# A two-block sequence mixer on one core: the weight loads issued by ScalarE instead of SyncE

## The chip, the core and the metric

The kernel runs on one core of a Trainium2 chip. A core has TensorE (PE in the profile; its weight loads are PEld), VectorE (DVE), ScalarE (ACT), GpSimd (POOL) and SyncE (SP), which run their own instruction streams in order and wait for each other through semaphores. The metric is the device time of one execution in microseconds, from the kernel's launch to its end; the comparison uses the median of several executions.

## What the reference computes

The input x has 2048 positions of 1024 channels in float32. The first block normalizes it, projects it, runs a diagonal state-space scan on 512 channels and a short gated convolution on the other 512, projects back and adds. The second block is a bidirectional chunked state-space mixer with a Fourier branch, and then a gated feed-forward network of width 2816. Cut to its frame:

```python
def reference(x, ...):
    xn = rmsnorm(x, norm_gain)
    proj = xn @ w_in                                    # 1024 -> 3072
    y = concat([s5_mixer(u, ...) * silu(z), short_conv_mixer(h, b, c, conv_w) * silu(z2)])
    x = rmsnorm(x + y @ w_out, final_norm_gain)         # end of the first block
    hc = modulate(rms_norm(ctx, g), shift, scale)       # 256 positions of context
    _, hf, hb = ssd_bidir(conv7(hc @ w_in2), ...)       # its two final states
    hx = modulate(rms_norm(x, g), shift, scale)
    y = ssd_bidir(conv7(hx @ w_in2), ..., hf, hb)       # states and outputs, chunks of 128
    x = x + gm * rms_norm(concat([fourier_mix(uf), rms_norm(y * silu(z))]) @ w_out2)
    hx2 = modulate(rms_norm(x, g), shift, scale)
    return x + gf * rms_norm((silu(hx2 @ w_gate) * (hx2 @ w_up)) @ w_down)
```

## The kernel before

Activations lie with channels on the 128 partitions, in four blocks of 512 positions. Nearly all of the multiplying is done in tiles of 128 output channels by 512 positions. `mtile` makes such a tile: `weights` fetches a strip of the weight matrix (128 x 1024 float32, 512 KB; strips of `w_down` are narrower), and `gemm` multiplies it with eight strips of the activations. To keep float32 accuracy each operand is split into a high and a low part of TensorE's fp32r type: `whi` is ScalarE's rounding of the raw strip `wraw` (L112), `wlo` the remainder, computed by VectorE or, in some stages, by GpSimd (L115, chosen by `pool_lo`). A full tile is 24 matmuls in this order: sixteen that use `whi` (L126 with the high part of the activations, L127 with the low part), then eight that use `wlo` (L130). There are 634 strips in one execution.

The buffers around a strip set its pace. `wraw` has three buffers, `whi` and `wlo` two each. So the load of strip j can start once `wlo` of strip j-3 has been computed; the rounding of strip j once the L127 matmuls of strip j-2 are done; and `wlo` of strip j once its L130 matmuls are done. PSUM holds three buffers for these tiles (`mm`), two for small results (`nb`) and three for the state and scan products (`ss`).

The order of the work is not written out by hand. The Python code lists units of work (`a1_units`, `s5_units`, `b_units` and so on), `weave` and `merge` interleave them, and a scheduler then orders the instructions on each engine; `high_priority(offset=self.ahead)` lets it bring the three steps of `weights` forward by some 40 to 75 places. The stages that matter here, in the profiled execution:

- 0 to about 1090 us: the first block. Beside the weight tiles run the state-space parameters (many small DVE operations, tables `T` on POOL, stores of `Cd`, `Gd`, `Td`, `Md`) and the scan (`s5_units`), which loads those tables again.
- about 1090 to 1640 us: `b_units`, the projection of the second block, the seven-tap convolution and the chunk states. A chunk's states are four products on PE (L1125), each into an `ss` buffer; VectorE adds the first half into `hF` (L1299) and ScalarE copies the second half into `stB` (L1301). The fourth product needs the buffer of the first one again. Here `wlo` is computed by POOL for the first three of the four blocks.
- about 1640 us to the end: the attention-like part of the chunks, the output projection, and the feed-forward network, one block of positions woven into the next.

All 2037 transfers are issued by SyncE, in one line. Every transfer signals one of eight semaphores, which are taken in turn (`DMAHW0` to `DMAHW7` in the listings below), and a transfer waits for the one that used its semaphore before, unless that is known to have ended.

Of the kernel before, what the change touches and what calls it, by code (L numbers as in the profile page):

```python
# [61 lines left out]
class Kernel:  # L62
# [41 lines left out]
    def weights(self, src, pool=None, bufs=2):  # L104

        nc = self.nc
        n = src.shape[1]
        with self.tc.high_priority(offset=self.ahead):
            raw = self.t(self.wp, (P, n), "wraw", bufs=3)
            nc.sync.dma_start(out=raw, in_=src)  # L110
            hi = self.t(pool or self.wp, (P, n), "whi", F32R, bufs=bufs)
            nc.scalar.copy(hi, raw)  # L112
            lo = self.t(pool or self.wp, (P, n), "wlo", F32R, bufs=bufs)
            eng = nc.gpsimd if self.pool_lo else nc.vector
            eng.tensor_tensor(lo, raw, hi.bitcast(F32), ALU.subtract)  # L115
        return hi, lo
# [1841 lines left out]
```

## Time and profile before

| What | Value |
|---|---|
| time of three executions | 3629.4, 3638.18 and 3636.63 us, median 3636.63 us |
| profiled execution | 3634.7 us, of which its span from first to last instruction is 3632.8 us |
| mean granted clock of TensorE | 0.98 |
| busy share of the span | PE 95%, PEld 78%, DVE 59%, ACT 40%, POOL 27% |
| memory | 472.63 MB read, 112.36 MB written, 161 GB/s over the span |

The profiled execution lies 1.9 us below the median. A share of busy time is an average over stages with different limits, and issuing a transfer is not counted as busy.

### The profile page before, as it was taken

To read this page: it belongs to the slowest core of one execution; us is meant where nothing else is said; L and a number is where in the kernel's file an instruction comes from. 1 tells how busy PE (TensorE), PEld (TensorE's weight loads), DVE (VectorE), ACT (ScalarE), POOL (GpSimd) and SP (SyncE) were. 2 spreads that over 40 slices of the span, in tenths; PEclk is the share of its full clock that TensorE was granted. 3 is DMA by queue.
4 is the path that set the end of the run, shared out by engine and by line. 5 is a ranking of instruction groups with operands and counts; after the bars stand their busy time and mean duration, and the time that the engine had idled before them with its cause. 6 is when DMAs were issued, how large, how long until landed. Compare 5 with 4: busy or idle time off the path is not lost.

```text
span 3632.8 us, 46986 instructions
## 1 busy us (share of the span) xinstructions
PE 3462.0 (95%) x16602; PEld 2831.0 (78%) x16602; DVE 2147.9 (59%) x3991; ACT 1461.9 (40%) x2350; POOL 965.3 (27%) x931
## 2 busy tenths in 40 slices
PE   8899999988989999999999999999999999999998
PEld 6677888776778888876777788877888778887887
DVE  8765534446687577777756544566445664454334
ACT  3233232234444344335535533355333553343222
POOL 1764233232353453343213101131011220110001
PEclk9999999999989999999999999999999999999999
DMA  6467565677654565466554334443345443444232
GB/s 199 156 190 223 191 210 175 203 230 241 211 191 153 178 204 172 163 205 203 164 186 137 118 111 155 155 149 120 111 135 171 140 130 111 127 153 130 83 113 76
DMA packets 322508, 588.14 MB, mean 162 GB/s; under 512 B 73952, under 2 KB 150624, under 8 KB 321376
## 3 DMA queue, kind: packets, MB, share of 16 engines
q1 hardware_dynamic: 322272, 585.13, 51.1%
q8 instruction: 132, 2.16, 0.2%
q14 instruction: 104, 0.85, 0.1%
HBM read 472.63 MB, written 112.36 MB: 161 GB/s over the span
## 4 chain that ended last, share of the span: by engine, by line
PE 60%; DVE 6%; DMA 4%; ACT 2%; issue 1%; POOL 1%; SPq 0%; POOLq 0%; DVEq 0%; ACTq 0%
PE mm L130 17%; PE mm L126 17%; PE mm L127 17%; PE ss L1125 1%; PE nb L940 1%; PE ss L1473 1%; PE ss L1523 1%; DVE cy L1038 1%; DMA outT<-n_t 1%; PE nb L1501 1%; PE ss L1138 1%; PE mm L1149 1%; PE mm L1150 0%; PE mm L1151 0%; PE nb L192 0%
## 5 line engine op out<-in xcount | busy, mean ns | idle before, releaser
L112 ACT CAST whi<-wraw 128x1024 fp32r<-128x1024 f32 (+3 forms) x634 | 568.9, 898 | 1044.3 <-PE mm L127 758.0
L115 DVE TENSOR_TENSOR wlo<-wraw,whi 128x1024 fp32r<-128x1024 f32 (+3 forms) x516 | 538.2, 1044 | 698.2 <-PE mm L130 487.3
L126 PE MATMUL mm<-xh,whi 128*128 128x512 f32 (+1 forms) x2000 | 801.2, 403 | 49.4 <-ACT whi L112 30.1
L127 PE MATMUL mm<-xl,whi 128*128 128x512 f32 (+1 forms) x2000 | 787.8, 396 | 5.8 <-DVE xl L142 3.6
L152 POOL TENSOR_TENSOR n_acc<-n_acc,n_sq 128x512 f32<-128x512 f32 (+1 forms) x175 | 229.5, 1315 | 1365.5 <-ACT n_sq L151 1337.9
L126 PE MATMUL mm<-dxh,whi 128*128 128x512 f32 x1408 | 549.9, 391 | 1.7 <-ACT dxh L997 1.7
L127 PE MATMUL mm<-dxl,whi 128*128 128x512 f32 x1408 | 548.6, 390 | 1.6 <-DVE dxl L998 1.5
L130 PE MATMUL mm<-xh,wlo 128*128 128x512 f32 (+1 forms) x2000 | 500.2, 392 | 9.9 <-DVE wlo L115 9.6
L126 PEld LDWEIGHTS mm<-xh,whi 128*128 128x128 f32 x2000 | 385.7, 193 | 138.7 <-ACT whi L112 40.9
L127 PEld LDWEIGHTS mm<-xl,whi 128*128 128x128 f32 x2000 | 385.7, 193 | 86.1 <-DVE xl L142 6.6
L130 PEld LDWEIGHTS mm<-xh,wlo 128*128 128x128 f32 x2000 | 375.7, 191 | 89.9 <-DVE wlo L115 12.9
L115 POOL TENSOR_TENSOR wlo<-wraw,whi 128x1024 fp32r<-128x1024 f32 (+1 forms) x118 | 284.1, 2410 | 549.0 <-ACT whi L112 268.0
L130 PE MATMUL mm<-dxh,wlo 128*128 128x512 f32 x1408 | 349.7, 389 | 0.0
L126 PEld LDWEIGHTS mm<-dxh,whi 128*128 128x128 f32 x1408 | 264.1, 188 | 57.7 <-ACT dxh L997 3.0
L127 PEld LDWEIGHTS mm<-dxl,whi 128*128 128x128 f32 x1408 | 264.3, 188 | 57.2 <-DVE dxl L998 2.8
L130 PEld LDWEIGHTS mm<-dxh,wlo 128*128 128x128 f32 x1408 | 263.6, 188 | 54.3
L126 PE MATMUL mm<-hh,whi 128*128 128x512 f32 (+1 forms) x744 | 285.5, 390 | 5.0 <-ACT hh L141 4.7
L1038 DVE SCALAR_TENSOR_TENSOR cy<-mm,vecs,cy 128x504 f32<-128x504 f32 (+5 forms) x396 | 266.9, 690 | 27.6 <-ACT cy L1032 24.4
L127 PE MATMUL mm<-hl,whi 128*128 128x512 f32 (+1 forms) x744 | 280.5, 382 | 2.0 <-DVE hl L142 2.0
L130 PE MATMUL mm<-hh,wlo 128*128 128x512 f32 (+1 forms) x744 | 199.3, 383 | 0.0
L126 PEld LDWEIGHTS mm<-hh,whi 128*128 128x128 f32 x744 | 139.7, 189 | 36.7 <-ACT hh L141 9.4
L127 PEld LDWEIGHTS mm<-hl,whi 128*128 128x128 f32 x744 | 140.5, 189 | 30.4 <-DVE hl L142 5.2
(473 smaller groups left out, 4510.7 us busy)
## 6 DMA issues: line engine op xcount, KB each, us to landing
wraw<-w_in SPq DMA_DIRECT2D x186, 512.0 KB, 4.5
wraw<-w_gate SPq DMA_DIRECT2D x88, 512.0 KB, 3.7
wraw<-w_up SPq DMA_DIRECT2D x88, 512.0 KB, 3.6
wraw<-w_out SPq DMA_DIRECT2D x64, 512.0 KB, 3.9
mraw<-w_ada SPq DMA_DIRECT2D x96, 256.0 KB, 3.7
n_x<-xT SPq DMA_DIRECT2D x85, 256.0 KB, 4.7
n_x<-X1d SPq DMA_DIRECT2D x80, 256.0 KB, 4.0
n_x<-X2d SPq DMA_DIRECT2D x72, 256.0 KB, 4.0
```

The lines of the kernel that those rows point to most:

```text
L112: nc.scalar.copy(hi, raw)
L115: eng.tensor_tensor(lo, raw, hi.bitcast(F32), ALU.subtract)
L126: nc.tensor.matmul(ps, lhsT=hi[:, s], rhs=xh, start=k == ks[0], stop=False)
L127: nc.tensor.matmul(ps, lhsT=hi[:, s], rhs=xl, start=False, stop=False)
L130: nc.tensor.matmul(ps, lhsT=lo[:, s], rhs=rhs(k)[0], start=False, stop=k == ks[-1])
L152: nc.gpsimd.tensor_tensor(acc, acc, sq, ALU.add)
L940: nc.tensor.matmul(ps, lhsT=raws[k // 4][:, k % 4 * P:(k % 4 + 1) * P], rhs=sc[:, k, 0:n], start=k == 0, stop=k == KD - 1)
L1038: nc.vector.scalar_tensor_tensor(yr[:, :, lo:hi], pr[:, :, lo + d:hi + d], w(k), yr[:, :, lo:hi], ALU.mult, ALU.add)
L1125: nc.tensor.matmul(ps, lhsT=B_tm[:, c, g], rhs=xw[:, g].rearrange("p d r e -> p (d r e)"), start=True, stop=True)
L1138: nc.tensor.transpose(ps[:, c], src[:, c * P:(c + 1) * P], self.ident)
L1149: nc.tensor.matmul(ps, lhsT=ah, rhs=wh[:, s], start=(k == 0), stop=False)
L1473: nc.tensor.matmul(ps, lhsT=CT[:, g, c * P:(c + 1) * P], rhs=hFB[:, g].rearrange("p d e -> p (d e)"), start=True, stop=True)
```

## The change

One word of `weights`: the transfer of the raw strip is put into ScalarE's instruction stream instead of SyncE's. Nothing else in the source differs, and no buffer is added.

```diff
@@ -107,7 +107,7 @@
         n = src.shape[1]
         with self.tc.high_priority(offset=self.ahead):
             raw = self.t(self.wp, (P, n), "wraw", bufs=3)
-            nc.sync.dma_start(out=raw, in_=src)
+            nc.scalar.dma_start(out=raw, in_=src)
             hi = self.t(pool or self.wp, (P, n), "whi", F32R, bufs=bufs)
             nc.scalar.copy(hi, raw)
             lo = self.t(pool or self.wp, (P, n), "wlo", F32R, bufs=bufs)
```

The 634 strip loads leave SyncE's stream (2033 transfers in its listing before, 1401 now, four of them pieces of `w_uf` that use the same raw buffers) and enter ScalarE's. Since the scheduler decides again, the other engines' orders move too, most of all in the first fifth of the program. Three places, as the built programs list them; a row is line, operation, output<-inputs with buffer numbers, and size, and in brackets the semaphores that it waits for (named by the engine that signals them).

The first is the start of ScalarE's stream, as one piece of the difference. `n_x` and `n_t` are strips of x, `xh` their high parts, `sc` a small vector.

```order
-L329 ACT_TABLE_LOAD
-L329 ACTIVATE sc_6_104<-vecs_1_75 128x16
+L110 DMA wraw_47_220<-w_in 128x1024
+L110 DMA wraw_66_291<-w_in 128x1024
+L762 ACT_TABLE_LOAD
+L762 ACTIVATE xh_18_127<-n_x_22_131,vecs_1_75 128x512
 L112 CAST whi_48_222<-wraw_47_220 128x1024
-L762 ACTIVATE xh_18_127<-n_x_22_131,vecs_1_75 128x512
```

The function table that stood ahead of everything is replaced by another one, which stands with the first `xh`; the table and the vector `sc` that stood first now come six `xh` later. With its waits the new table load reads:

```order
L762 ACT_TABLE_LOAD [waits DMAHW2_49]
L762 ACTIVATE xh_18_127<-n_x_22_131,vecs_1_75 128x512 [waits DMAHW1_49]
L112 CAST whi_48_222<-wraw_47_220 128x1024 [waits DMAHW0_49]
```

So it stands behind a wait for a load from SyncE, where the old one waited for nothing.

The second place is in the first block, where the output projection begins. SyncE's stream before, with the load of strip 1242 between a store of the previous tile's sum (`X2d<-us`, which waits for DVE) and others:

```order
L698 DMA s5C_1217_6372<-Cd_98 128x1024 [waits DMAHW7_49,PE_49]
L700 DMA s5M_1218_6374<-Md_99 128x512
L199 DMA n_x_1220_6406<-xT 128x512 [waits DMAHW2_49,DMAHW1_49,DVE_49]
L902 DMA X2d_87<-us_1215_6366 128x512 [waits DVE_49]
L110 DMA wraw_1242_6513<-w_out 128x1024 [waits DMAHW3_49,Pool_49]
```

And ScalarE's stream of the change around the same load:

```order
L884 ACTIVATE hs_1188_6239<-mm_1187_6226,hb_glu_5_102 128x512 [waits Activation_49]
L110 DMA wraw_1228_6447<-w_out 128x1024 [waits DMAHW4_49,Pool_49]
L110 DMA wraw_1242_6513<-w_out 128x1024 [waits DMAHW6_49,Pool_49]
L141 CAST xh_1131_5998<-zs_1189_6241 128x512 [waits DVE_49]
L112 CAST whi_1222_6410<-wraw_1221_6408 128x1024 [waits DMAHW5_49,PE_49]
```

The load no longer stands behind that store and those loads; it stands ahead of the rounding of an earlier strip, and waits for POOL (the `wlo` that frees its buffer) and for a semaphore.

The third place is a chunk's states, on ScalarE. Before:

```order
L112 CAST whi_2094_10568<-wraw_2093_10566 128x1024 [waits DMAHW5_49,PE_49,Pool_49]
L1032 ACTIVATE cy_2064_10427<-mm_2063_10402,vecs_1_75 128x512 [waits PE_49]
L1301 COPY stB_2069_10447<-ss_2070_10448 128x192 [waits DMAHW5_49,DVE_49,Activation_49]
L1301 COPY stB_2069_10447<-ss_2071_10452 128x192 [waits DVE_49]
L1301 COPY stB_2069_10447<-ss_2072_10456 128x192 [waits DVE_49]
```

Of the change:

```order
L112 CAST whi_2094_10568<-wraw_2093_10566 128x1024 [waits DMAHW5_49,PE_49]
L1032 ACTIVATE cy_2064_10427<-mm_2063_10402,vecs_1_75 128x512 [waits PE_49]
L110 DMA wraw_2150_10918<-w_in2 128x1024 [waits DMAHW7_49,Pool_49]
L1301 COPY stB_2069_10447<-ss_2070_10448 128x192 [waits DMAHW6_49,DVE_49]
L1301 COPY stB_2069_10447<-ss_2071_10452 128x192 [waits DVE_49]
```

A strip load that waits for POOL now stands ahead of the first of the four state copies. Of the 634 loads in ScalarE's stream 359 name one of the eight transfer semaphores among their waits.

## Rows read from the trace of the kernel before

**Rows 1.** The page: busy times of the engines, and the one transfer queue.

```profile
PE 3462.0 (95%) x16602; PEld 2831.0 (78%) x16602; DVE 2147.9 (59%) x3991; ACT 1461.9 (40%) x2350; POOL 965.3 (27%) x931
...
q1 hardware_dynamic: 322272, 585.13, 51.1%
...
PE 60%; DVE 6%; DMA 4%; ACT 2%; issue 1%; POOL 1%; SPq 0%; POOLq 0%; DVEq 0%; ACTq 0%
```

**Rows 2.** Stretch, length, busy PE PEld DVE ACT POOL, clock, transfers' share, GB/s.

```profile
0.00:1090.00 1090.00, 987.59 (x4834) 820.53 (x4834) 668.60 (x1354) 387.82 (x544) 428.07 (x387) 0.96 0.65 202
1090.00:1640.00 550.00, 537.10 (x2806) 444.44 (x2807) 388.27 (x759) 229.76 (x366) 221.51 (x235) 0.99 0.54 180
...
1816.00:3633.00 1817.00, 1773.39 (x8207) 1443.84 (x8206) 962.73 (x1630) 746.83 (x1233) 260.79 (x250) 0.99 0.42 131
```

**Rows 3.** Waits of PE: us in total, times, longest.

```profile
PE mm L126 <- ACT whi L112: 30.1, 17, 6.3
...
PE mm L130 <- DVE wlo L115: 9.6, 6, 3.5
...
PE ss L704 <- DMA s5M<-Md: 4.8, 3, 2.6
...
PE ss L660 <- DMA s5G<-Gd: 2.9, 2, 2.6
```

**Rows 4.** Waits of SyncE's queue: us in total, times, longest.

```profile
SPq L110 <- DVE wlo L115: 1188.2, 409, 6.8
SPq L110 <- POOL wlo L115: 154.3, 49, 8.8
```

**Rows 5.** Who waited for the strip loads of line 110: us, times.

```profile
  ACT whi L112: 159.0, 46
```

**Rows 6.** Timeline, POOL, SyncE and ACT, 736 to 763: start, us, instruction, [idle before].

```profile
736.80 2.37 POOL L115 TENSOR_TENSOR wlo<-wraw,whi 128x1024 fp32r<-128x1024 f32 x1 [4.33 <-ACT whi L112]
...
758.69 0.38 SPq L110 DMA_DIRECT2D wraw<-w_out  x1
...
762.96 1.04 ACT L112 CAST whi<-wraw 128x1024 fp32r<-128x1024 f32 x1 [2.96 <-DMA wraw<-w_out]
```

**Rows 7.** Timeline, PE: first and last of five waits for a late strip.

```profile
124.38 0.50 PE L126 MATMUL mm<-xh,whi 128*128 128x512 f32 x1 [0.96 <-ACT whi L112]
...
764.05 0.50 PE L126 MATMUL mm<-xh,whi 128*128 128x512 f32 x1 [1.21 <-ACT whi L112]
```

**Rows 8.** Busy times and granted clock (third column from the end) around one of them.

```profile
139.00:143.00 4.00, 2.13 (x9) 1.42 (x8) 4.00 (x7) 0.79 (x1) 3.58 (x6) 1.00 0.93 281
143.10:146.50 3.40, 3.19 (x8) 2.51 (x9) 3.40 (x6) 0.67 (x2) 3.16 (x6) 0.50 0.68 237
```

**Rows 9.** Timeline of a chunk's states, 1210 to 1213, and the last of eight such.

```profile
1210.06 2.36 POOL L115 TENSOR_TENSOR wlo<-wraw,whi 128x1024 fp32r<-128x1024 f32 x1 [1.03 <-ACT whi L112]
1211.04 0.32 ACT L1301 COPY stB<-ss 128x192 f32<-128x192 f32 x1 [0.30 <-DVE hF L1299]
1212.45 0.33 SPq L110 DMA_DIRECT2D wraw<-w_in  x1
...
1469.43 0.32 ACT L1301 COPY stB<-ss 128x192 f32<-128x192 f32 x1 [0.30 <-DVE hF L1299]
...
1470.83 0.33 SPq L110 DMA_DIRECT2D wraw<-w_in  x1
```

**Rows 10.** Timeline of the start: ACT, SyncE, PE.

```profile
0.74 1.28 ACT L329 ACT_TABLE_LOAD   x1 [0.74 <-PEq L1949]
1.18 0.42 SPq L110 DMA_DIRECT2D wraw<-w_in  x1
1.65 0.42 SPq L761 DMA_DIRECT2D n_x<-xT  x1
...
6.73 0.72 ACT L762 ACTIVATE xh<-n_x,vecs 128x512 fp32r<-128x512 f32 x1 [0.62 <-DMA n_x<-xT]
...
7.50 0.80 PE L126 MATMUL mm<-xh,whi 128*128 128x512 f32 x1 [7.50 <-ACT xh L762]
```

## The prediction, made before the change was run

> **What bounds the kernel now.** I read the page first. PE is busy 3462.0 of 3632.8 us, and the chain that ended last lies on PE for 60% and on SyncE's issuing for 0% [rows 1]. So the change can win only in the 171 us in which PE stands still, plus what the clock loses after such pauses. The windows show where that is [rows 2]: before 1090 us PE is idle for 102 us (1090.00 less 987.59), from 1090 to 1640 for 13 us, from 1816 to the end for 44 us in 1817. The clock is 0.96 in the first stretch and 0.99 in the others. What a pause does to the clock is seen around one of them: up to 143 us the granted clock is 1.00, PE then waits 2.18 us for a late strip, and over the next 3.4 us it is 0.50, 1.2 instead of 2.4 GHz [rows 8]. Work that takes 1.7 us at full clock takes 3.4 there, so a pause of one or two microseconds may cost 1.7 more.
>
> Next, the waits. PE waits 30.1 us for `whi` (17 times) and 9.6 us for `wlo` (6 times) [rows 3]. That is 39.7 us, and all that better strip loads could ever take away directly, whatever the reasons of those waits are. On SyncE the loads stand 1188.2 + 154.3 us in line until `wlo` has freed a raw buffer [rows 4]. That sounds like much, but SyncE has no other work, and ScalarE waited only 159.0 us for all strips together, in 46 of 634 cases [rows 5]. At most 17 of those reached PE.
>
> **What the change gives: strips that were late behind SyncE's line.** The second listing shows the pattern. Strip 1242's buffer was free at 736.80 + 2.37 = 739.2 us, but its load stood behind a store that waited for DVE and was issued only at 758.69. ScalarE could round it at 762.96 and waited 2.96 us for it [rows 6], and PE had to wait until 764.05, 1.21 us [rows 7]. I followed each of PE's waits for `whi` and `wlo` back in this way. Five are of this kind, the first at 124.38 and the last at 764.05 [rows 7], with 0.96, 2.18, 2.48, 1.34 and 1.21 us. That is 8.17 us. The others end on ScalarE's, VectorE's or POOL's own work, and an earlier load would not shorten them. In the changed order loads no longer stand behind stores. Term: **-8.2 us**. From the one side it is bounded by 0 (another instruction of ScalarE's takes the store's place), from the other by 8.2 + 5 x 1.7 = 16.7 us, if each of the five pauses carries a half-clock stretch with it. I take the bare pauses, because ScalarE's stream has waits of its own ahead of these loads.
>
> Line 704 and line 660 wait 4.8 + 2.9 = 7.7 us for tables that SyncE loads behind other rows [rows 3]. Those loads and the stores ahead of them all stay on SyncE, so I take 0; if the strip loads were what held them up, 7.7 us more are won.
>
> **What the change costs: ScalarE waits in line.** The third listing shows it. While `wlo` is on POOL, a load that waits for POOL now stands ahead of the first copy of the state products (line 1301). Before, that copy ran at 1211.04, while POOL's `wlo` ended at 1210.06 + 2.36 = 1212.42 and SyncE issued the load at 1212.45 for 0.33 us [rows 9]. If ScalarE must issue it first, the copy runs at 1212.78, which is 1.74 us later. The copy frees the `ss` buffer that the fourth product of line 1125 needs, so PE stops there. There are eight such places in the changed order, the first at 1211.04 and the last at 1469.43 (1470.83 + 0.33 - 1469.43 = 1.73) [rows 9]. Worked out in the same way, five give 1.74, one 1.57 and two 0.90 us. That is 12.1 us. Term: **+12.1 us**. Lower bound 0: PE may reach the fourth product later than the copy for reasons that are hidden now, or POOL may run ahead when its loads come sooner. Upper bound 12.1 + 8 x 1.7 = 25.7 us, if each pause also halves the clock as in [rows 8]. I take the bare pauses, because most of these are shorter than the 2.18 us there.
>
> **The start.** Before, a table load of 1.28 us at 0.74 us was hidden, since ScalarE had nothing to do until 5.06 us; the first `xh` ran at 6.73, when its load had landed, and PE began with it at 7.50 [rows 10]. Now the table load waits for that landing too, so `xh` comes 1.28 us later. Against that, SyncE issues `n_x` first, at 1.18 instead of 1.65 us, 0.47 sooner. A second load, which I price by the same row at 1.28 us, stands between later `xh`, on which PE still lives. Term: 1.28 + 1.28 - 0.47 = **+2.1 us**. Bounds: 0, if both are made up in the first microseconds, and 2.6 without the earlier issue.
>
> **Issuing itself.** 634 loads at 0.33 us [rows 9] are 209 us that ScalarE now spends. In the last stretch it is busy 746.83 of 1817 us [rows 2], and some 390 loads add about 129, less than half of its time in all. The cover is this idle time, and PE's lead of one to two strips. Where the cover is gone, at PE's 17 waits for `whi` [rows 3], the cost is 17 x 0.33 = 5.6 us. I take 0 and keep 5.6 for the range. A gain is possible here too, and it is in the first term.
>
> 359 of ScalarE's loads also wait for a shared semaphore that another transfer has to give back. No trace here shows what a wait of that kind costs on ScalarE. Below it is nothing, since the transfer before it is usually long past. Above, I take the five places of [rows 7] again, now caused by ScalarE waiting for a slow store of SyncE's, for 8.2 us. I take 0, since the load of strip j has seven or more transfers between it and that one, and keep 8.2 for the range.
>
> **A rule to set against this.** The page shows one hardware queue with a busy share of 51.1% [rows 1], and what SyncE loses at these loads is 1342 us of waiting in line, against 209 us of issuing [rows 4, 9]. The Trainium skill, "DMA: Bandwidth & Descriptors", section "Issuing engines are not separate DMA queues", says that transfers started by several engines run on the same 16 DMA engines and interleave, so that spreading them saves only the sequencer's time of issue, usually small. By that rule the sum would be 0. No run here shows yet whether the loads get through faster. The five places of [rows 7] are not about issuing time, which is why my sum has a gain in it all the same.
>
> **The sum.** 3634.7 - 8.2 + 12.1 + 2.1 = 3640.7 us for an execution like the profiled one. The median of the runs shown is 1.9 us higher, so I put the time at 3642.6, say **3643 us**, 0.2% above before. A measurement can tell about 0.3% (11 us) from no change, so this is: no difference to be measured.
>
> **The rivals.**
> *ScalarE becomes the one that waits (slower).* The eight places cost their full 25.7 us, the start 2.1, and the five pauses remain because ScalarE reaches those loads late too: 3636.6 + 27.8 = **3664 us**. It decides if PE's fourth product waits for line 1301 at all eight places and the granted clock falls behind it; it is already slower than the bound if 9 us of these 25.7 come true without the gain. For it speaks that the in-order position is certain and POOL's `wlo` ends after the copy in the trace. Against it: PE's idle time in that stretch is small now (13 us) [rows 2], so there is some lead there.
>
> *SyncE's line was what cost (faster).* Strips come on time in the first stretch, with the clock (16.7), the scan's tables too (7.7), and the state places are absorbed: 3636.6 - 24.4 + 2.1 = **3614 us**. For it speaks that most of PE's idle time, 102 us, lies where the strips stand behind stores [rows 2, 6]. Against it: only five waits are traced to it, and ScalarE is in order as well.
>
> *Nothing changes.* The 1342 us of waiting were all covered, ScalarE has time enough, and both terms vanish: **3637 us**. For it speaks the 0% of SyncE in the chain [rows 1].
>
> **Chances.** My forecast 0.28, nothing 0.12, slower 0.33, faster 0.27. The forecast and "nothing" are within 0.3%: 0.40. The slower case has more than the faster one, because its cause is to be seen in the order, while the gain needs ScalarE to be on time. The range takes in both rivals and the unknown costs of issuing, shared semaphores (5.6 + 8.2) only in part: **3606 to 3674 us**. The forecast's own range is 3626 to 3648.
>
> **What would show it.** Right: PE's waits for `whi` before 1090 us fall by about 8 us, and the five places are gone; at eight places between 1211 and 1470 us PE waits for line 1301 on `ss`, 12 us in all; PE begins near 8.3 us; the last stretch keeps its 1773 us of PE in 1817. Wrong: line 1125 never waits for ScalarE; ScalarE shows long stops at line 110 before 1090 us, followed by PE waiting for `xh` or `whi`; the clock of the middle stretch falls under 0.99. Most of all I would be wrong if ScalarE's stops at line 110 delay its evictions of `mm`, for PE would then wait at places that the trace before does not have.

## The result, and the profile after

The change made the kernel slower: 3672.16 us (median of 4, 3667.04 to 3675.25) against 3635.78 us (median of 4, 3629.4 to 3638.18). The ratio is 1.0101, with a 95% interval from 1.0083 to 1.012, about 36 us. The profiled execution has a span of 3668.6 us and a mean clock of 0.972.

The page of the changed kernel: busy times, the transfer queues, and the chain by engine. They answer to [rows 1].

```profile
PE 3467.7 (95%) x16602; PEld 2839.9 (77%) x16602; DVE 2155.4 (59%) x3991; ACT 1456.9 (40%) x2351; POOL 958.5 (26%) x931
...
q1 hardware_dynamic: 230976, 311.41, 27.1%
q10 hardware_dynamic: 91296, 273.72, 23.4%
...
PE 45%; DVE 1%; ACT 1%; DMA 1%; issue 0%; POOL 0%; POOLq 0%; DVEq 0%; ACTq 0%
```

The busy times are those of before within 10 us, so the work is the same, and 36 us more of the span are idle time and the clock. The chain's shares can't be compared: they sum to 74% before and 48% now, since the chain could be followed back only to 941 us there and to 1901 us here. So neither chain says anything of the first 900 us. The strip loads now have a hardware queue of their own. The two shares, 27.1 and 23.4, add up to 50.5% where one queue had 51.1%, so the transfers themselves take as long as before.

To find the place I counted the roundings (line 112) by their starts, from zero, and compared the start of the k-th in each trace with the same one before. The 15th is 1.8 us late, the 30th (at 219 us before) 29.2, the 45th (at 313) 22.4, the 90th (658) 24.3, the 120th (864) 42.1, the 150th (1028) 50.0. From there it goes down slowly, to 36.5 for the last. So the whole loss lies in the first block, in two steps: one in the table stage, up to 220 us, and one in the scan and the output projection, between 660 and 1030. All of these are differences of one execution from another, and executions of one kernel differ by some us. The last 8 us, between the 135th (42.3) and the 150th, at the seam of the blocks, come in other runs too that lose nothing in the end.

PE's waits (us in total, times, longest). One row of the kernel before, which [rows 3] doesn't have:

```profile
PE ss L1125 <- ACT stB L1301: 3.2, 1, 3.2
```

The changed kernel:

```profile
PE mm L126 <- ACT whi L112: 43.4, 10, 10.2
PE mm L126 <- ACT xh L141: 22.0, 5, 8.8
...
PE mm L126 <- ACT yh L872: 11.1, 3, 9.6
...
PE mm L126 <- DVE us L900: 6.0, 1, 6.0
...
PE ss L1125 <- ACT stB L1301: 4.0, 2, 3.6
...
PE ss L660 <- DMA s5G<-Gd: 3.8, 2, 2.2
PE ss L704 <- DMA s5M<-Md: 3.6, 2, 2.9
```

Beside [rows 3], `whi` has fewer waits (10 for 17), but longer ones. Waits for `xh` and `yh` of 8 to 10 us are new. Line 1125, where I had put 12 us, waits 4.0 us (3.2 before). Lines 660 and 704 wait 7.4 us for the scan's tables, 7.7 before, so that term was 0 as I had taken it.

SyncE's waits (same columns), which answer to [rows 4]:

```profile
SPq L1612 <- DMA wraw<-w_down: 358.8, 3, 119.7
...
SPq L624 <- POOL T L413: 85.2, 8, 17.7
...
SPq L712 <- DMA wraw<-w_in: 55.1, 13, 10.7
...
SPq L951 <- DMA wraw<-w_in: 37.3, 7, 6.6
...
SPq L712 <- DMA wraw<-w_glu: 12.2, 3, 5.7
...
SPq L712 <- DMA wraw<-w_out: 10.4, 4, 3.7
```

This is what the change brought. SyncE no longer loads strips, but its other transfers wait for strip loads to land: the scan's stores of `Yd` (line 712) alone 77.7 us in 20 places. Line 712 doesn't use strips. What it needs is one of the eight semaphores, and a strip load in ScalarE's stream was the last to take it. Matching each transfer with the one before it on its semaphore gives 182.5 us in 47 such stops of SyncE before 1090 us, and 36.3 us in 6 stops of ScalarE at line 110 for transfers of SyncE's, before 250 us. (The expectations below go by a narrower count, 170 us in 43 and 38 us in 8.) Before the change SyncE's came to 6.8 us in 9 places.

The sum of such stops is not their price. Behind 1090 us SyncE stands for strips still longer, 657 us in 11 places, nearly all of it at four stores: the row of line 1612 above, and 280.5 us at line 1693. There the data that the store has to write came 22 to 40 us after the semaphore, so these stops cost nothing. What counts is a stop ahead of a transfer that PE will soon need.

**One such loop, whole.** Timeline of the changed kernel, SyncE, ACT and PE, at a store of `Yd` in 16 pieces (start, us, instruction, idle before it):

```profile
839.42 14.12 SPq L712 DMA_DIRECT2D Yd<-Yg  x16
...
840.98 0.39 ACTq L110 DMA_DIRECT2D wraw<-w_out  x1
...
848.50 0.33 ACTq L110 DMA_DIRECT2D wraw<-w_out  x1
...
854.27 0.34 ACTq L110 DMA_DIRECT2D wraw<-w_out  x1
857.62 0.34 SPq L199 DMA_DIRECT2D n_x<-YCd  x1
...
861.18 0.62 ACT L141 CAST xh<-n_x 128x512 fp32r<-128x512 f32 x1 [7.68 <-DMA n_x<-YCd]
...
865.09 1.22 PE L126 MATMUL mm<-xh,whi 128*128 128x512 f32 x2 [8.83 <-ACT xh L141]
```

The same place before:

```profile
802.24 7.66 SPq L712 DMA_DIRECT2D Yd<-Yg  x16
...
811.43 0.37 SPq L199 DMA_DIRECT2D n_x<-YCd  x1
...
818.30 0.51 PE L126 MATMUL mm<-xh,whi 128*128 128x512 f32 x1 [3.03 <-ACT xh L141]
```

The 16 pieces go twice around the eight semaphores. Inside the store SyncE stands 2.56 us for the strip issued at 840.98 and 3.40 for that of 848.50, and behind it 4.08 us for that of 854.27, each until the strip has landed. The store takes 14.12 us, not 7.66, and `n_x` is issued 18.2 us after the store's start, not 9.2. `xh` comes late, and PE waits 8.83 us where it waited 3.03 (there ScalarE had been waiting for VectorE, not for `n_x`). The strip loads for which SyncE stands had themselves waited for `wlo`, and `wlo` waits for PE. So a PE that falls behind holds up its own next input.

PE has three more waits of 6 us and over between 363 and 1090 us:

```profile
559.34 0.80 PE L126 MATMUL mm<-xh,whi 128*128 128x512 f32 x1 [8.19 <-ACT xh L141]
...
744.29 0.80 PE L126 MATMUL mm<-yh,whi 128*128 128x512 f32 x1 [9.57 <-ACT yh L872]
...
819.71 0.76 PE L126 MATMUL mm<-xh,whi 128*128 128x512 f32 x1 [6.02 <-DVE us L900]
```

Each of them follows a load (of `n_x`, or at 819.71 of a table `s5T`) that SyncE issued late because it, or a store of `Yd` ahead of it, had stood for a strip. The four come to 32.6 us. Before, PE's longest waits between 363 and 1090 us were 6.5 us, at line 1149, and 5.9 us for `n_acc`, and no other was over 4 us.

**The other direction**, in the table stage, where ScalarE stands for SyncE's transfers:

```profile
200.99 0.33 SPq L624 DMA_DIRECT2D Td<-T  x1
...
203.70 0.33 ACTq L110 DMA_DIRECT2D wraw<-w_in  x1
204.14 0.63 ACT L789 ACTIVATE zs<-zs 128x512 f32<-128x512 f32 x1 [10.08 <-DMA Td<-T]
204.68 1.03 ACT L112 CAST whi<-wraw 128x1024 fp32r<-128x1024 f32 x1
...
205.76 0.75 PE L126 MATMUL mm<-xh,whi 128*128 128x512 f32 x1 [2.95 <-ACT whi L112]
```

The load at 203.70 waits for the semaphore of a store of `Td`, and that store had waited in SyncE's line for POOL to finish the table. ScalarE is idle for 10.08 us, with a rounding that PE needs behind the load. The largest stop of this kind, 12.8 us, ends at 150.0: the load waits for the semaphore of a store of `Cd`, which had stood in SyncE's line behind one of `Td`. PE waits 6.85 us for the rounding behind that load:

```profile
150.06 0.33 ACTq L110 DMA_DIRECT2D wraw<-w_in  x1
...
151.59 0.79 PE L126 MATMUL mm<-xh,whi 128*128 128x512 f32 x1 [6.85 <-ACT whi L112]
...
244.80 0.79 PE L126 MATMUL mm<-xh,whi 128*128 128x512 f32 x1 [8.03 <-ACT whi L112]
```

The wait at 244.80 is of another kind: ScalarE stood 14.21 us until a store of `Ud` had freed a buffer, and that store stood behind one of `Td` in SyncE's own line. No shared semaphore has a part in it.

### The profile page after: what moved, and what is told of

Same layout as the page of the kernel before. It is cut to its first block, busy times and chain, and to the rows that moved or that the text cites. A ratio compares the mean times of both kernels' runs of the same rounds, so it can differ in the third digit from the quotient of the medians.

```text
span 3668.6 us, 46906 instructions
## 1 busy us (share of the span) xinstructions
PE 3467.7 (95%) x16602; PEld 2839.9 (77%) x16602; DVE 2155.4 (59%) x3991; ACT 1456.9 (40%) x2351; POOL 958.5 (26%) x931
## 3 DMA queue, kind: packets, MB, share of 16 engines
q1 hardware_dynamic: 230976, 311.41, 27.1%
q10 hardware_dynamic: 91296, 273.72, 23.4%
## 5 line engine op out<-in xcount | busy, mean ns | idle before, releaser
L152 POOL TENSOR_TENSOR n_acc<-n_acc,n_sq 128x512 f32<-128x512 f32 (+1 forms) x175 | 245.8, 1408 | 1384.3 <-ACT n_sq L151 1346.4
L130 PEld LDWEIGHTS mm<-xh,wlo 128*128 128x128 f32 x2000 | 375.5, 192 | 89.3 <-DVE wlo L115 12.1
```

Source lines behind the costliest of these rows:

```text
L130: nc.tensor.matmul(ps, lhsT=lo[:, s], rhs=rhs(k)[0], start=False, stop=k == ks[-1])
L152: nc.gpsimd.tensor_tensor(acc, acc, sq, ALU.add)
```

## The experiments

Theory T: the two streams hold each other up through the semaphores they share. Rival L: ScalarE is late because it stands in line for `wlo`. Rival O: the scheduler's other order costs, not the loads. In the diffs `where` is a letter that is set at the borders of the stages: "a" the table stage, "s" the scan (from some 320 to 790 us), "r" the rest of the first block, "b" and "d" the second block. The last two columns are how much later the 45th and the 150th rounding start than before.

| Run | Strip loads issued by | Median, us | Ratio to before, interval | 45th | 150th |
|---|---|---|---|---|---|
| the change | ScalarE | 3672.16 | 1.0101 (1.0083 to 1.012) | 22.4 | 50.0 |
| e1_first_block | ScalarE in the first block | 3677.8 | 1.0115 (1.0083 to 1.0147) | 19.7 | 49.4 |
| e2_second_block | ScalarE in the second block | 3631.54 | 0.9996 (0.9981 to 1.0012) | -1.0 | 12.1 |
| e6_pool_scan | ScalarE, POOL in the scan | 3667.05 | 1.009 (1.0058 to 1.0123) | 19.1 | 36.6 |
| e7_mark_only | SyncE, ScalarE stands in line too | 3653.02 | 1.0052 (1.0037 to 1.0068) | 1.1 | 6.9 |
| e8_after_tables | ScalarE in "s" and "r" | 3656.39 | 1.0077 (1.0055 to 1.0099) | -1.3 | 26.7 |
| e9_stores_pool | ScalarE; `Yd` stores on POOL | 3630.57 | 1.0003 (0.9992 to 1.0014) | 18.6 | 9.2 |
| e11_stores_pool_before | SyncE; `Yd` stores on POOL | 3608.61 | 0.9948 (0.9932 to 0.9964) | -1.6 | -20.1 |
| e3_pool_scan_only | SyncE, POOL in the scan | 3621.52 | 0.998 (0.9967 to 0.9992) | -2.2 | -4.4 |
| e12_both_pool | ScalarE; `Yd`, `Td` stores on POOL | 3638.05 | 1.0017 (1.0007 to 1.0026) | 23.1 | 18.7 |
| e13_both_pool_before | SyncE; `Yd`, `Td` stores on POOL | 3641.57 | 1.0021 (1.0011 to 1.003) | 24.5 | 13.0 |
| e14_late_both_pool | as e13, ScalarE from the scan on | 3641.47 | 1.0025 (1.0009 to 1.004) | 24.3 | 17.1 |
| e15_late_stores_pool | as e11, ScalarE from the scan on | 3605.36 | 0.9931 (0.9913 to 0.9948) | -1.1 | -12.3 |

**Where the loss is.** In the first run ScalarE issues the loads of the first block alone:

```diff
-            nc.scalar.dma_start(out=raw, in_=src)
+            (nc.scalar if self.where in "asr" else nc.sync).dma_start(out=raw, in_=src)
```

> Loads on ScalarE only in the first block, on SyncE from the second block on. In the trace after the change the 150th rounding is 50 us behind before, the 165th to 240th 47 to 49, and the last 36.6: the first block loses 50, the rest gives 13 back. Theory T (two streams that share eight semaphores hold each other up, only before 1090 us: SyncE stood 170 us for loads that ScalarE had not got through, ScalarE 38 us for SyncE's transfers): the loss stays whole, 3636 + 48 = about 3684 us. Rival L (ScalarE in line: wherever it stands for wlo at line 110, its own work comes late): about half, since 234 us of its stops lie before 1090 and 357 behind: some 3655. Rival O (the scheduler's other order of everything, not the loads): no forecast, any size.

The loss is whole, 3677.8 us. In the second run `where in "bd"` picks ScalarE:

> Loads on SyncE in the first block, on ScalarE from the second block on. T: nothing is shared in a harmful way there, since SyncE stood 3 us and ScalarE not at all for the other's semaphores, so the 13 us that were given back remain: 3636 - 13 = about 3623 us. L: ScalarE's 357 us of stops for wlo behind 1090 us cost, 3636 + 15 or more. My prediction's own place, the chunk states with +12 to +26 us: PE would wait there for line 1301; in the trace after the change it does so for 4.0 us in all, as before (3.2), so I expect nothing from it.

No difference, and 13 us were not won. In its trace the rows gain from the 150th rounding (12.1 late) to the last (2.3 early), but 8.8 us are lost first, between the 135th and the 150th, at the seam of the blocks. ScalarE stands some 400 us for `wlo` behind 1090 us in this run without cost, which speaks against L. The expectation's "3 us" leaves out the long stops of SyncE at lines 1612 and 1693: they are here too (358.9 and 280.6 us), and this run is where they are seen to cost nothing.

**Is it ScalarE's standing in line?** Loads on SyncE; ScalarE writes one column of the buffer first, and so waits for it in the same way:

```diff
-            nc.sync.dma_start(out=raw, in_=src)
+            nc.scalar.copy(raw[:, :1], self.vecs[:, :1]); nc.sync.dma_start(out=raw, in_=src)
```

> Loads stay on SyncE as before, but ScalarE writes one column of each raw buffer just before its load, so that ScalarE stands in line for the buffer (its wait for wlo) as in the change, with some 0.2 us of work, and issues nothing. What it leaves out: nothing, the load overwrites the column. T: ScalarE's waiting for wlo is not the cost and no new stream shares the semaphores, so it is near before, 3636 to 3650 us (a load now also waits for ScalarE to come to it). L: the loss of the change is there, 3670 us or more, with PE waiting for ScalarE's xh and whi.

3653.02 us lies 3 us over T's range and 17 below L's. In the first block ScalarE stands 264.6 us in line for `wlo` here (238 us in the change); the change loses 50 us there, and this run is 6.9 late at the 150th rounding. So standing in line is not that loss. It does cost something later, in part at the chunk states:

```profile
PE ss L1125 <- ACT stB L1301: 10.3, 7, 3.2
```

That is my prediction's mechanism, in a kernel in which PE meets it.

**The scan.** POOL issues the loads where it computes `wlo`, the rest as in the change (`nc.gpsimd if self.where == "s" else nc.scalar`):

> As the change, but in the scan's stage (about 363 to 860 us, where POOL computes wlo) POOL issues the loads itself. Then a load waits in POOL's stream for POOL's own work, and ScalarE and SyncE have no strip loads there. T: SyncE's stops behind strip loads in that stage (about 145 us in 37 places) vanish, and with them PE's waits of 8.2 us at 559, 9.6 at 744 and 6.0 at 820: 3672 less 15 to 25, about 3652 us. O or contention between transfers: the waits stay, about 3672. If POOL's own issuing is slow, wlo comes late and PE waits for line 115: over 3672.

SyncE's stops for strip loads from 363 to 1090 us fell from 176 to 27 us, PE's wait at 559 is gone, and the 90th rounding is 10.4 us late instead of 24.3. But the time, 3667.05, can't be told from the change. The nine stops that are left are for strips of "r", from 783 us on, six of them at line 712, and from the 90th to the 150th rounding this run loses 26 us, as much as the change. PE's wait for `xh` of 8.8 us at 865 is still there, with 9.56 us at 849. So the expectation was missed, and the time alone agrees with the rival's 3672 us. The expectation counted stops, and those that cost are the few ahead of a late `n_x`.

In the next run ScalarE loads in "s" and "r" alone:

> Loads on ScalarE only from the scan to the end of the first block (about 363 to 1090 us), on SyncE in the first 363 us and from the second block on. In the first-block run the 45th rounding was 20 us behind before and the 150th 49. T: the first 363 us then lose nothing, and the scan and output projection still lose theirs, since SyncE still stands some 165 us for strip loads: 3633 + 25 = about 3658 us, with PE's long waits for xh and yh near 740 and 860 us still there. If the whole loss came from the table stage and only showed later: about 3633.

3656.39: the two steps add up (25 here, some 20 in the table stage, 42 to 45 in the run of the first block). The four long waits of PE return nearly to the tenth, 8.28, 9.57, 6.02 and 8.66 us, and SyncE's stops for strips between 363 and 1090 us are 176.5 us in 42 places. Then the stores of `Yd` go to POOL, whose transfers use other semaphores (`DMASW` in the listing), first in the change, then, as the control, in the kernel before:

```diff
-                        nc.sync.dma_start(
+                        nc.gpsimd.dma_start(
                             out=self.Yd[2 * tb + i, c0:c0 + 128, t, :].rearrange("(g h) k -> h g k", h=GH),
```

> As the change (all strip loads on ScalarE), but the scan's stores of Yd (line 712, 16 pieces each) are issued by POOL, whose transfers use other semaphores. T: those stores no longer wait for a strip load, and the loads of n_x behind them in SyncE's line come on time; SyncE's stops for strip loads fall from 170 to about 80 us (20 of the 43 were at line 712), and PE's waits of 9.6 us for yh at 744 and of 8.8 us for xh at 865 fall to 3 us or less: 3672 less 12 to 20, about 3656 us. If those waits came from the stores' length or from contention and not from the shared semaphores: they stay, about 3672 or more, since POOL has the stores in its line.

> The control for the run above: the kernel before (loads on SyncE) with the stores of line 712 on POOL. If the stores alone, whatever the semaphores, hold SyncE up, this is as much faster than before as the other is than the change: some 15 us. T: before, SyncE stood only 4 us for strip loads' semaphores from 363 to 1090 us, so there is little to win: 3633 within 6 us, or a little slower by POOL's issuing.

Both expectations were too small. Each measured against its own runs of the kernel before, the change goes from 36.4 us slower to 0.5 faster and gains 36.9 us, and the kernel before gains 22.5. So these 128 transfers cost 22 us on SyncE in any case, which I had not seen, and some 14 us more when the strip loads are on ScalarE. What they cost in the kernel before is not explained: SyncE stood there only 2.8 us for strips at line 712. The trace of the first shows the mechanism gone: no row of line 712 waits for a strip, SyncE's stops for strips between 363 and 1090 us are 9.2 us in 5 places, and of the four long waits of PE none is left (the longest for `xh` is 2.6 us), while the waits of the table stage stay:

```profile
PE mm L126 <- ACT whi L112: 44.9, 11, 10.4
...
PE mm L126 <- ACT xh L141: 4.5, 6, 2.6
...
L712 POOL DMA_DIRECT2D Yd<-Yg x128: 528/528/686, 411.3 to 812.6; - x128
```

Against its control this run is 20.2 us late at the 45th rounding and 21.2 at the 105th: from the scan on it loses nothing more up to there. At the 150th it is 29.3 late, by the 8 us of the seam, and at the last 22.7. The last run takes the table stage away as well:

```diff
-            nc.scalar.dma_start(out=raw, in_=src)
+            (nc.sync if self.where == "a" else nc.scalar).dma_start(out=raw, in_=src)
...
-                        nc.sync.dma_start(
+                        nc.gpsimd.dma_start(
                             out=self.Yd[2 * tb + i, c0:c0 + 128, t, :].rearrange("(g h) k -> h g k", h=GH),
```

> The change with two parts of it put right: the stores of Yd (line 712) on POOL, and the strip loads of the first 363 us back on SyncE; ScalarE issues all the others. With the stores alone the change took 3630.6 us, 22 more than the same kernel with all loads on SyncE (3608.6), and the 45th rounding was already 20 us behind there. T: the table stage holds all that was left of the loss, so this one comes to 3608 within 6 us, and no step of the lag is left from 363 us on; moving the loads gives nothing there either. If it stays over 3620: ScalarE's standing in line from 363 us on costs, and T is wrong on it. If it is under 3600: loads on ScalarE are of use once the coupling is gone, and it is the version to keep.

3605.36 us, as T said. It is 0.7% faster than the kernel before and 1.8% faster than the change, and by its interval it can't be told from the control with all loads on SyncE (0.9948). So ScalarE's issuing from the scan on costs nothing once the stores are elsewhere, and gains nothing: the same step that costs 25 us with the stores on SyncE. PE's four long waits are absent here too, though ScalarE still stands in line for `wlo`. The lag is not quite without a step: against the control it is 7.7 us at the 150th rounding, at the seam, and -0.3 at the last.

**Loads on POOL alone.** The kernel before, with POOL issuing the strips of the scan:

> The kernel before with one difference: in the scan's stage, where POOL computes wlo, POOL also issues the strip loads; SyncE issues the others. No stream then waits for another one's wlo, and the late strips of that stage come on time: PE's waits for whi between 363 and 860 us (1.34, 2.06, 3.31, 1.67, 1.82, 1.21 and 2.38 us, 13.8 in all before) vanish, with some half-clock stretches: 3633 less 10 to 20, about 3620 us. If the freed time only moves the wait to POOL's n_acc or to xh behind SyncE's stores, about 3633.

As expected, if at the lower end (7 to 10 us faster): 3621.52, and of PE's 16.0 us for `whi` between 363 and 860 us none is left among its costlier waits. Those for `xh` (7.3 us) and `yh` (5.0) now lead the list of that stretch.

**The table stage: not settled.** Here `Td`, for which SyncE waits, goes to POOL too, with ScalarE's loads, with SyncE's, and with ScalarE's from the scan on:

> As the change with the stores of Yd on POOL (3630.6 us), and the stores of the tables Td (line 624) on POOL too, which computes them. With Yd alone the loss of the first 363 us was still whole (the 45th rounding 20 us behind the same kernel with loads on SyncE). T: what ScalarE waits for there are transfers that stand behind Td in SyncE's line, which waits for POOL (85 us in 8 places); without Td in that line ScalarE's stops for SyncE's semaphores fall from 38 to under 10 us and the 45th rounding is at most 8 us behind (4 of them from the start): 3630 - 14 = about 3616 us. Rival O (the other order of the first stage costs, not the waits): the 45th stays 20 us behind, 3630.

> Control: the kernel before (loads on SyncE) with the stores of Yd and Td on POOL. With Yd alone it took 3608.6 us. SyncE waited 56 us for POOL's T before, with strip loads behind it; PE's waits of 2.18 us at 143 and 2.48 at 279 are of that kind. So 0 to 6 us less: about 3605.

> The control above with one difference: from the scan on (after about 363 us) ScalarE issues the strip loads. T: with Yd off SyncE's line nothing is shared in a harmful way after 363 us, so moving the loads neither costs nor, as in the run with the second block alone, gives anything: the control within 6 us, about 3605. If loads on ScalarE are of use once the coupling is gone (late strips behind SyncE's line): 3595. L (ScalarE standing in line for wlo costs): 3615 or more.

All three came out slower than expected. The first lowered ScalarE's stops for SyncE's semaphores before 363 us from 34.3 (with the `Yd` stores alone) to 1.5 us, as T said, and yet it is 23 us late at the 45th rounding. The reason has nothing to do with the loads, since the control has it too:

```profile
202.77 0.63 ACT L151 ACTIVATE n_sq<-n_x 128x512 f32<-128x512 f32 x1 [53.67 <-POOL n_acc L152]
...
207.28 1.03 ACT L112 CAST whi<-wraw 128x1024 fp32r<-128x1024 f32 x1
...
208.36 0.79 PE L126 MATMUL mm<-xh,whi 128*128 128x512 f32 x1 [56.26 <-ACT whi L112]
```

POOL, with the stores in its stream, computes tables before it gets to `n_acc`. ScalarE waits 53.67 us for it with a rounding behind, and PE 56.26 (43.55 in the first of the three). Next to such a stop a smaller one doesn't show. The three runs take 3638 to 3642 us, so where the loads are issued makes no difference there, but they don't tell T from O in this stage.

## Why the prediction came out as it did

The time lies within the range, at its upper end, but the forecast, no measurable difference, was wrong. That the range holds it is luck: its upper end was made for the slower rival, whose 3664 us is near the measured time, and whose mechanism, the chunk states, is not what happened.

**The step that failed** is the shared semaphores. I wrote that 359 of ScalarE's loads wait for one, bounded that by 8.2 us and took 0, because seven other transfers lie between a load and the one it waits for. That holds in one stream, where those seven have been issued before. Between two streams it doesn't: each runs ahead until it meets a semaphore that the other, standing for something else, has not come to. The term, taken at 0 and bounded by 8.2 us, measured 36 us of ScalarE's stops and 182 us of SyncE's. In PE's time it is the loss of the scan and output projection, 25 us by e8_after_tables. Moving the `Yd` stores takes 14 us of it away in the change, and all of it in the pair with the table stage on SyncE (e8_after_tables against e15_late_stores_pool). To it comes some part of the 20 us of the table stage. That SyncE could come to wait for ScalarE I had not considered at all. "SyncE has no other work" is the sentence that hid it: it has 1403 other transfers, among them every `n_x`. And the 0% of SyncE in the chain, which I took for a sign that nothing would change, was no evidence, since that chain begins at 941 us.

**The gain was there, and larger.** From 363 to 1090 us PE waited for `whi`, first before and then after the change (us, times, longest):

```profile
PE mm L126 <- ACT whi L112: 16.3, 10, 3.3
...
PE mm L126 <- ACT whi L112: 1.0, 2, 0.5
```

My five places gave 8.2 us in all, two of them in this stretch. So the other waits there, which I had put down to the engines' own work, went too, as they did in e3_pool_scan_only. The gain was given back as waits for `xh`, `yh` and `us` in the same stretch (22.0, 11.1 and 6.0 us, against 5.6 and 2.5 for `xh` and `yh`).

**The chunk states: the copy came late, and PE did not wait.** Timeline of the changed kernel at one of them:

```profile
1256.95 2.10 PE L1125 MATMUL ss<-xw,B_tm 128*128 128x384 f32 x6
1257.34 2.36 POOL L115 TENSOR_TENSOR wlo<-wraw,whi 128x1024 fp32r<-128x1024 f32 x1 [0.22 <-POOL xw L1117]
...
1258.88 1.84 PE L940 MATMUL nb<-sc,mraw 128*128 128x1 f32 x16
...
1259.74 0.33 ACTq L110 DMA_DIRECT2D wraw<-w_in  x1
...
1260.17 0.76 ACT L1301 COPY stB<-ss 128x192 f32<-128x192 f32 x3 [2.24 <-DVE hF L1299]
...
1261.60 0.81 PE L1125 MATMUL ss<-xw,B_tm 128*128 128x384 f32 x2
```

The load waits for POOL's `wlo`, which ends at 1259.70, and the first copy comes behind it, 2.0 us after VectorE's part of that product had ended at 1258.15. This is the kind of stop that I had worked out from [rows 9] (1.74 us there). But the scheduler has put other matmuls (line 940 and the next tile's) between the third product and the fourth, so that PE has work meanwhile. I read the change's order on ScalarE and took PE's from before. The 12.1 us were 0.8 (4.0 less 3.2).

**The start** cost about what I said, by luck. PE begins at 10.22 us instead of 7.50, 2.7 us later, for 2.1 predicted:

```profile
1.18 0.42 SPq L761 DMA_DIRECT2D n_x<-xT  x1
...
7.22 1.28 ACT L762 ACT_TABLE_LOAD   x1 [7.22 <-DMA n_x<-xT]
8.52 0.72 ACT L762 ACTIVATE xh<-n_x,vecs 128x512 fp32r<-128x512 f32 x1
...
9.14 1.03 ACT L112 CAST whi<-wraw 128x1024 fp32r<-128x1024 f32 x1
...
10.22 0.80 PE L126 MATMUL mm<-xh,whi 128*128 128x512 f32 x1 [10.22 <-ACT whi L112]
```

`n_x` was issued at 1.18 us as I had worked out, but it landed later than before, not sooner (some 0.5 us). The table load adds its 1.28. The remaining 0.9 us I had not seen, though the first listing shows it: the first rounding, which ran at 5.06 us before, now stands behind `xh`, and PE begins when that rounding is done. The second table load, my other 1.28 us, has no part in PE's beginning. By the 15th rounding 1.8 us are left of it.

**Issuing** is covered: 0.33 us each, and the second block with all its loads on ScalarE takes the same time.

**The rule I weighed.** The Trainium skill, "DMA: Bandwidth & Descriptors", section "Issuing engines are not separate DMA queues", says that it matters little which engine starts a transfer, since all run on the same 16 DMA engines. On the transfers this trace agrees: a strip lands 3.5 us after its issue (median) where it was 3.6, and the shares add up to the same. On the time it would have given no change. The 36 us came from what the rule doesn't speak of, the waits ahead of an issue.

**What stays open.** In the table stage it is open how the 20 us divide between ScalarE's stops and SyncE's own new order. Read from the trace, shared semaphores lie behind PE's waits at 151.59 and 205.76, 9.8 us together, and SyncE's order behind the 8.03 us at 244.80; that is a reading, and no run shows it. With ScalarE only standing in line, or with the loads on SyncE in that stage, nothing is lost, but no run took the semaphores alone away. Nor did one from 363 us on: each run has an order of its own, and rival O is excluded there only as far as the traces go (the four waits, each behind a stop that ends as a strip lands, back in e8_after_tables and gone with the stores). The 13 us that come back in the second block are not traced; PE's waits there for ScalarE's `E` of line 1504 fall by only 3.7 us.

## What to carry to other kernels

Splitting transfers over two instruction streams doesn't make them independent if they share completion semaphores. Before doing it, list for each stream what the earlier user of each semaphore waits for, in both directions, and above all for the rows ahead of the transfer that feeds the busiest engine. Then look at short stores in many pieces: here 128 of them, moved out of SyncE's stream to POOL's, gave more (22 us) than anything done with the 634 large loads (7 to 10 us), though no run shows which part of it is the semaphores and which the place in line. And weigh a stop by what stands behind it: 657 us of them cost nothing here, and four waits of PE made up the second step. And where a copy is late by the order of one engine, read the changed order of the engine that waits for it before charging it.

## What had not been expected of the hardware

ScalarE's issues show as a second hardware queue, but the 16 DMA engines' share is unchanged (27.1 and 23.4% for 51.1%). Issuing took 0.33 us on ScalarE as on SyncE, and on POOL 0.53 us for the `Yd` pieces, with its time counted as busy.
